# A hybrid retention and attention layer: half of the prompt's gate projections moved from the retention's end into the attention's entry

## The chip, the cores and the metric

The kernel runs on one core of a Trainium2 chip. The metric is the device time of one execution in microseconds (us). TensorE (PE) multiplies matrices, VectorE (DVE), ScalarE (ACT) and GpSimd (POOL) do the elementwise work, and SyncE (SP) issues most of the DMAs. Each engine takes its own instructions strictly in the order in which they were written for it, and stops at the first one whose operands or buffer are not ready.

## The reference, cut to what matters

Two sequences, a sample of 512 tokens and a prompt of 1024, go through the same layer with the same weights:

```python
h = rms_norm(x, norm_g) * (1 + scale) + shift
rq, rk, rv, rg, aq, ak, av, ag = split(h @ w_in)   # 4 x 512, then 512, 128, 128, 512 columns
ret_out = bidirectional_retention(rope(rq), rope(rk), rv)          # 4 heads of 128, chunks of 128
att_out = blocked_gqa(rope(norm(aq)), rope(norm(ak)), av)          # 8 query heads, 2 key heads of 64
mixed = concat([ret_out * silu(rg), att_out * silu(ag)]) @ w_out
y = x + gate * mixed
```

The columns `ag` are the attention's gates. The kernel computes them transposed: a 128-row tile of gate columns by 512 tokens at a time.

## The kernel before, in words

Everything is float32. A product is made of three fast matmuls on operands that are split in a high part and a remainder (`mm3`, lines 148 to 151: high by high, high by low, low by high). A weight is therefore loaded raw by DMA, cast to its high part on ACT (L139), and its remainder is made by a subtract on DVE or POOL (L140). `load_w` does this for 256 columns in four pieces; the tiles stand in a ring of two (`wring`).

`sequence` is called for the sample (nt = 4 query tiles of 128) and then for the prompt (nt = 8). For the prompt it runs through these stages:

1. Four retention heads. Head h's projections are woven with the core of head h-1 (`ret_core`: state sums `pst`, transposes `pk`/`pq`, scores `psc`, outputs `po`, then `pm`, the transposes of the normalised result, once per block of 512 tokens). The last head's core has no following head; it is woven with the attention's gate projections, `gates(rp, "rt1")`. These are 192 matmuls into the banks `pag`, in two weight tiles (`jj`) by two groups of 512 tokens (`g`) by two banks. After each bank comes `silu_gate`: a tanh on ACT (L362) and a combining step on DVE (L363). The results stay in `gs`, and are read in `normalise`.
2. `kvq_units`: keys, values and the first queries (`pkv`, `paq`). Then `ln_tables()` (L305) loads the activation tables that hold both logarithm and exponential, after the last tanh written so far.
3. The entry into the attention: the work of the attention is a list of steps in rounds (half-steps, eight per query tile), and the steps before round `turn` are woven with `q_rest`, which projects the remaining queries (`paq`). When the entry ends, the pools of the weights and of the normalised input are released and the DMAs of the output weights `wo` start into that memory (`read_wo`, at round `turn`).
4. The steady attention, eight query tiles of eight rounds. `st_unit`: scores `pT`, then their exponential `p` on ACT (L925), then row sums on DVE and POOL (L930, L933). `nat_units`: scores `pn` of the tile ahead, whose row maxima DVE takes (L870). `pv_pair`: `po`. After a tile, `normalise`: the logarithm (L962) and the exponential (L963) of the row sums on ACT, the product with the gates on DVE (L968, L969). Then `gate_out` splits the result into `Mh` and `Ml`, and sixteen `out_step`s of three matmuls each (bank `py`) multiply the tile with `wo`. The out-projection of one tile is the filler of PE during the attention of the next.

The order on each engine is the order of the code after weaving; within a round a priority sorts the steps. `weave(units, n, steps, m, lead)` takes one unit and then as many steps as keep the two lists level.

The lines that the change touches are the order of the queries (`qorder`, L338), `gates` (L760 to 777), its call beside the last core (L804), `turn` (L1025), the rounds of `gate_out` and `out_step` (L1054, L1061), and the weave of the entry's second part (L1094).

Of the kernel before, what the change touches and what calls it, by code (L numbers as in the profile page):

```python
# [37 lines left out]
PLEAD = 3  # L38
# [42 lines left out]
def hybrid_layer_kernel(ctx: ExitStack, tc: tile.TileContext, a: dict, y_prompt: bass.AP, y_sample: bass.AP):  # L81
# [23 lines left out]
    def slot(name):  # L105
        return slots.tile([P, 1024], F32, tag="slot", name=name)
# [46 lines left out]
    def load_w(wring, name, segs, wpool=None):  # L153
        w = (wpool or wring).tile([P, KD, 2, 256], F32R, tag="w", name=name)
        for _ in load_w_steps(wring, w, name, segs):
            pass
        return w
# [116 lines left out]
    def iter_steps(fns):  # L274
        for fn in fns:
            fn()
            yield

    def weave(units, n, steps, m, lead=0):
        done = 0  # L280
        for i, _ in enumerate(units):
            while steps is not None and done * (n - lead) < (i + 1 - lead) * m:
                if next(steps, steps) is steps:
                    steps = None
                done += 1
        if steps is not None:
            for _ in steps:
                pass
# [27 lines left out]
    def sequence(r, nt, first):  # L316
        tg = "ps"[r]
        ng = nt // 4
        ntok = nt * P
        x_in, y_out = xs[r], ys[r]  # L320
        with ExitStack() as sctx:
# [13 lines left out]
            order = [2 * tp + i for tp in tps for i in range(2)]  # L335
            kv = {}
            QPRE = hpair if first else 1
            qorder = [(half, tp) for half in range(2) for tp in tps[:QPRE]] + [(half, tp) for tp in tps[QPRE:] for half in range(2)]  # L338

            def open_kv():  # L340
                kvp = sctx.enter_context(pool(f"kv{tg}", bufs=1, reuse_waits="tile"))
# [156 lines left out]
            with ExitStack() as rctx:  # L498
# [258 lines left out]
                        S.mul(mT[:, h, b * 512 : (b + 1) * 512], pm2, gnT[:, h : h + 1])  # L757
                        yield

                def gates(pl, tag):  # L760
                    gs.extend(slot(f"g{tg}{i}") for i in range(2 * ng))
                    for jj in range(2):
                        segs = [(2816 + v * 256 + (2 * jj + i) * DH, DH) for i in range(2) for v in range(2)]
                        w = load_w(wring, f"wg{tg}{jj}", segs)
                        for g in range(ng):
                            for i in range(2):
                                pj = bank(f"pag{tg}{g}{jj}{i}")
                                wc = slice(i * P, (i + 1) * P)
                                c = slice(i * 512, (i + 1) * 512)
                                for k in range(KD):  # L770
                                    mm3(pj, w[:, k, 0, wc], w[:, k, 1, wc], hh[g][:, k, :], hl[g][:, k, :],
                                        k == 0, k == KD - 1)
                                    if k == 3:
                                        yield
                                silu_gate(pl, gs[g * 2 + jj][:, c], pj, [512], f"a{tg}{g}{jj}{i}", tag, 1)
                                yield
# [18 lines left out]
                for h in range(RH + 1):  # L795
                    if h < RH:
                        sls = [slot(f"s{tg}{h}_{i}") for i in range(nt // 2)]
                        units, n = head_units(h, sls), 2 * nt
                    else:
                        wctx.close()  # L800
                        if first:
                            units, n = kvq_units(rctx.enter_context(pool(f"pa{tg}", bufs=2, reuse_waits="tile"))), 2 * nt
                        else:
                            units, n = gates(rp, "rt1"), 8 * ng  # L804
                    extra, m = itertools.islice(gsteps, GSTEPS.get(h, 0)) if first else iter(()), nsteps
                    if first:
                        m += GSTEPS.get(h, 0)
                    weave(units, n, merge(prev, nsteps, extra, m - nsteps), m + ((2, 3)[r] if h == RH else 0))
                    if h == 0:
                        decay_tables()  # L810
                    if first and h < RH:
                        for j in range(sum(WOH[:h]), sum(WOH[: h + 1])):
                            with tc.issue_after(acts["w"].ins):
                                split_wo(wst, j)
                    if h < RH:
                        prev = ret_core(h, sls)
# [162 lines left out]
            def gate_out(t):  # L979
                d = st8[t]  # L980
                if "Mh" not in d:
                    gate_ret(t)
                o, Mh, Ml = d["o"], d["Mh"], d["Ml"]
                split(S.copy, V, Mh[:, 4:8, :], Ml[:, 4:8, :], o.rearrange("p (j q) -> p j q", j=4))
# [37 lines left out]
                        nc.gpsimd.dma_start(y_out[t * P : (t + 1) * P, :], x)  # L1022


            per_ = turn = nt  # L1025
            rounds = {}

            def at_round(rd, prio, fn):
                rounds.setdefault(rd, []).append((prio, fn))

            for n, t in enumerate(order):
                b = n * per_
                hb = b - per_
                prev = st8[order[0]] if n == 1 else {}
                if n:
                    at_round(hb - nt // 2, 8, lambda t=t: prep_split(t))
                    at_round(hb - 1, 6, lambda t=t: prep_T(t))
                if nt == 4:
                    for h in range(QH):
                        at_round(hb + h // 2, 4, lambda t=t, h=h, prev=prev: nat_head(t, h, prev))  # L1040
                else:
                    for k, units, paired in NATS:
                        at_round(hb + k, 4, lambda t=t, z=units, y=paired, prev=prev: nat_units(t, z, y, prev))
                for v in range(2):
                    at_round(b - 2 + v, 7.5, lambda t=t, v=v: fill_q2(t, v))
                    at_round(b - nt // 2 if v == 0 else b - 1, 7, lambda t=t, v=v: mid(t, v))
                    at_round(b - 1 + v, 2.5 if v else 5, lambda t=t, v=v: mid_t(t, v))
                for u in range(nt):
                    at_round(b + u, 1, lambda t=t, u=u: st_unit(t, u))
                    if u % 2:  # L1050
                        at_round(b + 4 * (u // 4 + 1), 3, lambda t=t, u=u: pv_pair(t, u // 2))
                at_round(b + per_, 3.2, lambda t=t: row_sums(t))
                at_round(b + per_, 8.5, lambda t=t: normalise(t))
                at_round(b + per_ + 1, 9, lambda t=t: gate_out(t))  # L1054
                if t == final:
                    at_round(b + per_ - 2, 9, lambda t=t: gate_ret(t))
                    at_round(b + per_ + 1, 10, lambda: final_steps(0))
                    at_round(b + per_ + 2, 10, lambda: final_steps(4))
                    continue
                for u in range(16):  # L1060
                    rd = b + per_ + 3 + u * nt // 16  # L1061
                    at_round(rd if first else min(rd, nt * per_), 0.5 if rd < nt * per_ or first else 4, lambda t=t, u=u: out_step(t, u))
            if first:
                def ahead():
# [10 lines left out]
            with ExitStack() as bctx:  # L1075
                ra = run_rounds_list(rounds, -100, turn)
                if first:
                    pools["at"] = sctx.enter_context(pool(f"at{tg}", bufs=2, reuse_waits="tile"))
                    pb = bctx.enter_context(pool(f"pb{tg}", bufs=2, reuse_waits="tile"))
                    prep_split(order[0])  # L1080
                    prep_T(order[0])
                    weave(itertools.chain(q_rest(pb, tps[hpair], hpair), gates(pb, "tg")), 4 * (nt // 2 - QPRE) + 8 * ng,
                          iter_steps(ra), len(ra), LEAD)
                else:
                    nb = sum(len(rounds[rd]) for rd in rounds if rd < PTURN)
                    with pool(f"pb0{tg}", bufs=2, reuse_waits="tile") as pb:
                        prep_split(order[0])
                        prep_T(order[0])
                        weave(q_rest(pb, tps[QPRE], hpair - QPRE), 4 * (hpair - QPRE), iter_steps(ra[:nb]), nb + 1)
                    hpools.pop().release()  # L1090
                    pools["q2"] = sctx.enter_context(pool(f"q2{tg}", bufs=1, reuse_waits="tile"))
                    pools["at"] = sctx.enter_context(pool(f"at{tg}", bufs=2, reuse_waits="tile"))
                    pb = bctx.enter_context(pool(f"pb{tg}", bufs=2, reuse_waits="tile"))
                    weave(q_rest(pb, tps[hpair], hpair), 4 * hpair, iter_steps(ra[nb:]), len(ra) - nb, PLEAD)  # L1094
                if first:
                    ln_tables()
            for p_ in reversed(hpools):
# [37 lines left out]
```

## Time and profile before

| | |
|---|---|
| time of three runs | 959.77, 952.63, 959.35 us (median 959.35) |
| the profiled execution | 954.35 us, of which the span from first to last instruction is 952.4 |
| busy in the span | PE 912.2 us (96%), DVE 546.5 (57%), POOL 396.1 (42%), ACT 336.7 (35%) |
| TensorE's granted clock | 0.992 of full speed on average |

A row of the timeline gives the start, the duration, the engine, the line, the operation, what it writes and reads, the count, and in brackets how long the engine stood idle before it and what ended that. The instructions of PE overlap; the distance between two starts is what one costs (0.23 us for a 512-column matmul whose own duration reads 0.39). An L number is a line of the kernel before; after the change, lines behind 338 stand one lower on the page, and those behind some 800 two lower.

### The profile page before, as it was taken

To read this page: it belongs to the slowest core of one execution; us is meant where nothing else is said; L and a number is where in the kernel's file an instruction comes from. 1 tells how busy PE (TensorE), PEld (TensorE's weight loads), DVE (VectorE), ACT (ScalarE), POOL (GpSimd) and SP (SyncE) were. 2 spreads that over 40 slices of the span, in tenths; PEclk is the share of its full clock that TensorE was granted. 3 is DMA by queue.
4 is the path that set the end of the run, shared out by engine and by line. 5 is a ranking of instruction groups with operands and counts; after the bars stand their busy time and mean duration, and the time that the engine had idled before them with its cause. 6 is when DMAs were issued, how large, how long until landed. Compare 5 with 4: busy or idle time off the path is not lost. (4 is left out here: it accounts for less than half of the span.)

```text
span 952.4 us, 15494 instructions
## 1 busy us (share of the span) xinstructions
PE 912.2 (96%) x6177; PEld 763.5 (80%) x6177; DVE 546.5 (57%) x972; ACT 336.7 (35%) x582; POOL 396.1 (42%) x346
## 2 busy tenths in 40 slices
PE   4899898999999999999999999999999999999998
PEld 2789798997676799999999998899965656665666
DVE  2475556677753493443525443245887878786833
ACT  3352232343535452232222232233143434343331
POOL 4233354455437673232302211035575546453551
PEclk9999999999999999999999999999999999999999
DMA  9964778214742521111002110110017011101111
GB/s 266 272 202 144 250 214 298 72 46 139 287 159 74 182 85 45 45 45 45 24 22 46 45 45 26 45 51 7 12 45 331 5 41 44 45 23 45 45 45 44
DMA packets 95683, 92.98 MB, mean 98 GB/s; under 512 B 23502, under 2 KB 84858, under 8 KB 92540
## 3 DMA queue, kind: packets, MB, share of 16 engines
q1 hardware_dynamic: 92876, 77.85, 26.8%
q0 software_dynamic: 2736, 14.16, 3.7%
q8 instruction: 48, 0.79, 0.4%
q14 instruction: 23, 0.19, 0.1%
HBM read 77.30 MB, written 14.68 MB: 97 GB/s over the span
## 5 line engine op out<-in xcount | busy, mean ns | idle before, releaser
L925 ACT ACTIVATE pp<-pTp 128x1024 f32<-128x1024 f32 x64 | 65.6, 1026 | 118.8 <-PE pTp L922 100.4
L870 DVE TENSOR_REDUCE nmhp<-pnp 128x2 f32<-128x1024 f32 x64 | 75.5, 1215 | 38.4 <-PE pnp L865 38.4
L933 POOL TENSOR_TENSOR accp<-accp,pp 128x512 f32<-128x512 f32 x48 | 64.9, 1351 | 19.9 <-ACT pp L925 18.3
L149 PE MATMUL pvgp<-wvgp,hhp 128*128 128x256 f32 x224 | 65.0, 290 | 0.0
L149 PE MATMUL pqkp<-wqkp,hhp 128*128 128x256 f32 x224 | 64.6, 288 | 0.0
L150 PE MATMUL pvgp<-wvgp,hhp 128*128 128x256 f32 x224 | 64.3, 287 | 0.0
L151 PE MATMUL pvgp<-wvgp,hlp 128*128 128x256 f32 x224 | 63.9, 285 | 0.0
L151 PE MATMUL pqkp<-wqkp,hlp 128*128 128x256 f32 x224 | 63.6, 284 | 0.0
L150 PE MATMUL pqkp<-wqkp,hhp 128*128 128x256 f32 x224 | 63.3, 283 | 0.0
L942 PE MATMUL pop<-pp,VVp 128*64 128x512 f32 x256 | 58.7, 599 | 0.0
L149 PE MATMUL pyp<-wo,Mhp 128*128 128x512 f32 (+1 forms) x136 | 53.9, 396 | 0.2 <-DVE ygp L1019 0.2
L150 PE MATMUL pyp<-wo,Mhp 128*128 128x512 f32 (+1 forms) x136 | 51.7, 380 | 0.0
L151 PE MATMUL pyp<-wo,Mlp 128*128 128x512 f32 (+1 forms) x136 | 51.6, 379 | 0.0
L933 DVE TENSOR_TENSOR accp<-accp,pp 128x512 f32<-128x512 f32 x48 | 42.7, 890 | 14.5 <-ACT pp L925 14.0
L637 POOL TENSOR_TENSOR sp<-rt1p,rt2p 128x512 f32<-128x512 f32 x16 | 22.9, 1428 | 57.1 <-DVE rt2p L634 57.1
L911 PE MATMUL pTp<-Q1Tp,kkp 128*128 128x512 f32 x128 | 41.4, 404 | 1.6 <-DVE nmhp L870 1.6
L942 PEld LDWEIGHTS pop<-pp,VVp 128*64 128x64 f32 x256 | 16.9, 136 | 32.4 <-issue 29.4
L149 PEld LDWEIGHTS pqkp<-wqkp,hhp 128*128 128x128 f32 x224 | 42.8, 191 | 0.0
L150 PEld LDWEIGHTS pqkp<-wqkp,hhp 128*128 128x128 f32 x224 | 42.8, 191 | 0.0
L149 PEld LDWEIGHTS pvgp<-wvgp,hhp 128*128 128x128 f32 x224 | 42.7, 191 | 0.0
L151 PEld LDWEIGHTS pqkp<-wqkp,hlp 128*128 128x128 f32 x224 | 42.7, 191 | 0.0
L150 PEld LDWEIGHTS pvgp<-wvgp,hhp 128*128 128x128 f32 x224 | 42.7, 191 | 0.0
(456 smaller groups left out, 2857.3 us busy)
## 6 DMA issues: line engine op xcount, KB each, us to landing
wo<-wod SPq DMA_DIRECT2D x16, 1024.0 KB, 14.7
wa<-in_w_ada_dram SPq DMA_DIRECT2D x16, 512.0 KB, 6.6
wod<-woz POOLq DMA_DIRECT2D x8, 1024.0 KB, 6.4
gr<-in_w_ada_dram SPq DMA_DIRECT2D x16, 256.0 KB, 5.0
xn<-in_x_prompt_dram SPq DMA_DIRECT2D x8, 512.0 KB, 7.6
xrp<-in_x_prompt_dram SPq DMA_DIRECT2D x8, 512.0 KB, 3.8
out_dram<-xrp POOLq DMA_DIRECT2D x7, 512.0 KB, 3.0
xs<-in_x_sample_dram SPq DMA_DIRECT2D x4, 512.0 KB, 6.6
```

What stands on the lines that cost most here:

```text
L149: T.matmul(out, lh, rh, start=first, stop=False)
L150: T.matmul(out, lh, rl, start=False, stop=False)
L151: T.matmul(out, ll, rh, start=False, stop=last)
L637: G.tensor_tensor(qk, t1, t2, op=ALU.add)
L870: V.tensor_reduce(d["nmh"][:, n, 2 * pr : 2 * pr + 2], pn.rearrange("p (i k) -> p i k", i=2), AX.X, ALU.max, negate=True)
L911: T.matmul(pT[:, i * 512 : (i + 1) * 512], kk[v][:, kb], st8[t]["Q1T"][:, hs, :].rearrange("p h q -> p (h q)"), start=True, stop=False)
L925: d["exp", u] = S.activation(p, pT, AF.Exp)
L933: d["sum", v] = E.tensor_tensor(acc, acc, p[:, i * 512 : (i + 1) * 512], op=ALU.add)
L942: m = T.matmul(d["po"][v * DH : (v + 1) * DH, :], VV[:, 2 * kp + i, v, :], ps[v][:, i * 512 : (i + 1) * 512], start=(kp + i == 0), stop=(2 ...
```

## The change

The gate projections of the prompt's first 512 tokens (group 0) leave the retention's end: `gates` takes a list of groups, the call beside the last core keeps group 1, and a second call for group 0 follows `q_rest` in the entry's weave. Since the weight tiles in the ring have been overwritten by then, the second call loads them again. The entry runs to round 11 instead of 8, with the start of `wo`, the first `gate_out` and all `out_step`s of the prompt three rounds later. The order of the second half's queries changes so that one weight tile is done with before the other, which frees its place in the ring.

```diff
+            qorder = [(half, tp) for half in range(2) for tp in tps[:QPRE]] + [(half, tp) for tp in tps[QPRE:hpair] for half in range(2)]
+            qorder += [(half, tp) for half in range(2) for tp in tps[hpair:]] if not first else [(half, tp) for tp in tps[hpair:] for half in range(2)]
...
-                def gates(pl, tag):
-                    gs.extend(slot(f"g{tg}{i}") for i in range(2 * ng))
+                def gates(pl, tag, groups=range(ng)):
+                    if not gs:
+                        gs.extend(slot(f"g{tg}{i}") for i in range(2 * ng))
...
-                        w = load_w(wring, f"wg{tg}{jj}", segs)
-                        for g in range(ng):
+                        w = load_w(wring, f"wg{tg}{jj}{groups[0]}", segs)
+                        for g in groups:
...
-                            units, n = gates(rp, "rt1"), 8 * ng
+                            units, n = gates(rp, "rt1", range(1, ng)), 8 * (ng - 1)
...
-            per_ = turn = nt
+            per_ = nt
+            turn = nt if first else nt + 3
...
-                at_round(b + per_ + 1, 9, lambda t=t: gate_out(t))
+                at_round(max(b + per_ + 1, turn), 9, lambda t=t: gate_out(t))
...
-                    rd = b + per_ + 3 + u * nt // 16
+                    rd = b + per_ + (3 if first else 6) + u * nt // 16
...
-                    weave(q_rest(pb, tps[hpair], hpair), 4 * hpair, iter_steps(ra[nb:]), len(ra) - nb, PLEAD)
+                    weave(itertools.chain(q_rest(pb, tps[hpair], hpair), gates(pb, "tg", range(1))), 4 * hpair + 8, iter_steps(ra[nb:]), len(ra) - nb, PLEAD)
```

Three places show how the instructions move. The first is PE at the retention's end, block 0 of the last head. Before, between the last output product `pop_0` and the first transpose `pmp_0` of the normalised block stand 25 gate matmuls:

```order
L739 MATMUL pop_0_6385<-R1p_6231,qd1p_0_6348 128x128
L739 MATMUL pop_0_6385<-sp_1_5537,sTp_0_6370 128x128
L151 MATMUL pagp_6372<-hhp_3527,wgp_6188 128x512
L149 MATMUL pagp_6454<-hhp_3526,wgp_6425 128x512
...
L151 MATMUL pagp_6454<-hhp_3526,wgp_6425 128x512
L501 MATMUL pmp_0_6467<-identr,mxp_0_6405 128x128
L501 MATMUL pkp_1_6488<-identr,sp_2_5538 128x128 x2
```

After the change they follow each other directly:

```order
L740 MATMUL pop_0_6344<-R1p_6231,qd1p_0_6320 128x128
L740 MATMUL pop_0_6344<-sp_1_5537,sTp_0_6327 128x128
L502 MATMUL pmp_0_6411<-identr,mxp_0_6364 128x128
L502 MATMUL pkp_1_6417<-identr,sp_2_5538 128x128 x2
L502 MATMUL pkp_1_6417<-identr,sp_3_5539 128x128 x2
```

For block 1, four gate matmuls stand between `pop_1` and `pmp_1` where there were ten.

The second place is ACT in a steady tile, around the logarithm and the exponential of the row sums. Before:

```order
L948 COPY op_8737<-pop_8610 128x512
L962 ACTIVATE pLp_8739<-pLp_8739 128x512
L963 ACTIVATE pLp_8739<-pLp_8739 128x512
L925 ACTIVATE pp_8766<-pTp_8761 128x1024
L139 CAST Mhp_8994<-mTp 128x512
```

After the change, each of the two has a table load ahead of it:

```order
L950 COPY op_9207<-pop_9093 128x512
L964 ACT_TABLE_LOAD
L964 ACTIVATE pLp_9209<-pLp_9209 128x512
L965 ACT_TABLE_LOAD
L965 ACTIVATE pLp_9209<-pLp_9209 128x512
L927 ACTIVATE pp_9231<-pTp_9226 128x1024
```

This is so in all eight tiles of the prompt, and one more load stands ahead of the first tanh in the entry: 17 loads that the program did not have.

The third place is PE behind the last gate matmul in the entry (`pag`, line 149 to 151). After the change 23 rows of the attention alone stand between it and the first out-projection `pyp`; these are the first six and the last three:

```order
L151 MATMUL pagp_7861<-hhp_3526,wgp_7765 128x512
L913 MATMUL pTp_7905<-Q1Tp_7480,kkp_6522 128x512 x2
L924 MATMUL pTp_7905<-Q2Tp_7821,k2p_6524 128x512 x2
L913 MATMUL pTp_7913<-Q1Tp_7480,kkp_6521 128x512 x2
L924 MATMUL pTp_7913<-Q2Tp_7750,k2p_6523 128x512 x2
L867 MATMUL pnp_7922<-kkp_6521,Q1Tp_7816 128x512 x2
...
L913 MATMUL pTp_7999<-Q1Tp_7480,kkp_6522 128x512 x2
L924 MATMUL pTp_7999<-Q2Tp_7821,k2p_6524 128x512 x2
L149 MATMUL pyp_8012<-wo_7938,Mhp_7957 128x512
```

Before, the stretch of the attention without filler lies between the last query projection `paq` and the first `pyp`; the transposes `pnm` and `pq1` of the first two tiles lie in it:

```order
L151 MATMUL paqp_7668<-wqp_6969,hlp_3528 128x256
L865 MATMUL pnp_7731<-kkp_6634,Q1Tp_7551 128x512 x2
L911 MATMUL pTp_7779<-Q1Tp_7180,kkp_6634 128x512 x2
L922 MATMUL pTp_7779<-Q2Tp_7556,k2p_6636 128x512 x2
L887 MATMUL pnmp_7788<-identr,nmp_7553 4x128
L844 MATMUL pq1p_7791<-identr,Q1p_7710 128x128 x8
```

What moved: 96 rows of `pag` stand in the entry behind `paq`, and those transposes lie among them. Without filler stand the second half of the first tile's scores and the `pn` of the next, three rounds later than before.

## Rows read from the trace of the kernel before

**Rows 1.** The page, part 1: busy time of each engine, its share of the span.

```profile
PE 912.2 (96%) x6177; PEld 763.5 (80%) x6177; DVE 546.5 (57%) x972; ACT 336.7 (35%) x582; POOL 396.1 (42%) x346
```

**Rows 2.** Busy time by stage: retention's end, entry, steady attention; clock, DMA share, GB/s last.

```profile
559.30:616.80 57.50, 56.65 (x306) 48.14 (x305) 22.08 (x42) 15.76 (x30) 8.36 (x8) 1.00 0.16 48
655.00:711.00 56.00, 55.60 (x387) 46.54 (x386) 44.47 (x77) 14.31 (x20) 30.72 (x28) 1.00 0.03 8
731.00:933.00 202.00, 199.17 (x903) 125.57 (x902) 144.59 (x165) 80.19 (x100) 102.04 (x79) 1.00 0.11 38
```

**Rows 3.** Timeline of PE, block 1 at the retention's end.

```profile
607.22 0.39 PE L739 MATMUL pop<-sp,sTp 128*128 128x128 f32 x2
607.37 0.48 PE L151 MATMUL pagp<-hhp,wgp 128*128 128x512 f32 x1
...
609.30 0.40 PE L150 MATMUL pagp<-hlp,wgp 128*128 128x512 f32 x1
609.53 0.40 PE L151 MATMUL pagp<-hhp,wgp 128*128 128x512 f32 x1
610.78 0.33 PE L501 MATMUL pmp<-identr,mxp 128*128 128x128 f32 x1 [0.85 <-DVE mxp L748]
```

**Rows 4.** Timeline of ACT, DVE and POOL there: the chain from `pop` to `mxp`.

```profile
607.65 0.60 ACT L741 ACTIVATE sqp<-pop 128x512 f32<-128x512 f32 x1 [5.08 <-PE pop L739]
...
609.33 1.01 POOL L127 TENSOR_TENSOR r_retp<-m_retp,mhalf 128x4 f32<-128x4 f32 x1
...
610.38 1.13 DVE L748 SCALAR_TENSOR_TENSOR mxp<-pop,r_retp,sp 128x128 f32<-128x128 f32 x4 [1.42 <-POOL r_retp L127]
```

**Rows 5.** PE at the sample's retention end, and the busy times just behind.

```profile
159.17 0.49 PE L739 MATMUL pos<-R1s,qd1s 128*128 128x128 f32 x2 [3.02 <-DVE qd1s L716]
...
159.60:163.00 3.40, 3.40 (x18) 3.40 (x17) 2.18 (x4) 0.00 (x0) 0.59 (x1) 0.50 0.78 246
```

**Rows 6.** Timeline of PE in the entry and behind it: rows with idle before them; one stretch.

```profile
691.44 0.50 PE L865 MATMUL pnp<-kkp,Q1Tp 64*128 64x512 f32 x2 [0.35 <-DVE Q2Tp L888]
...
712.02 0.85 PE L844 MATMUL pq1p<-identr,Q1p 128*128 128x128 f32 x8 [0.43 <-DVE nmhp L870]
...
714.73 0.22 PE L887 MATMUL pnmp<-identr,nmp 128*4 128x128 f32 x1 [0.74 <-DVE nmp L882]
...
721.14 0.73 PE L911 MATMUL pTp<-Q1Tp,kkp 128*128 128x512 f32 x2 [1.09 <-DVE nmhp L870]
...
722.88 1.22 PE L911 MATMUL pTp<-Q1Tp,kkp 128*128 128x512 f32 x2 [0.52 <-DVE nmhp L870]
...
722.80:726.20 3.40, 3.32 (x8) 2.68 (x9) 3.37 (x6) 1.64 (x2) 1.44 (x2) 0.50 1.01 424
```

**Rows 7.** Groups by line between 559 and 711 us: the gate matmuls and one weight's preparation.

```profile
L149 PE MATMUL pagp<-hhp,wgp 128*128 128x512 f32 x64 | 26.0, 406 | 0.0
...
L140 DVE TENSOR_TENSOR wgp<-wgp1r,wgp 128x512 fp32r<-128x512 f32 x2 | 3.1, 1570 | 0.6 <-ACT wgp L139 0.6
...
L139 ACT CAST wgp<-wgp1r 128x512 fp32r<-128x512 f32 x4 | 2.2, 628 | 0.0
```

**Rows 8.** The page, parts 5 and 6: the row maxima; the output weights' issues, time to landing.

```profile
L870 DVE TENSOR_REDUCE nmhp<-pnp 128x2 f32<-128x1024 f32 x64 | 75.5, 1215 | 38.4 <-PE pnp L865 38.4
...
wo<-wod SPq DMA_DIRECT2D x16, 1024.0 KB, 14.7
```

**Rows 9.** Timeline of ACT around the prompt's one table load for the tanh.

```profile
360.71 1.28 ACT L362 ACT_TABLE_LOAD   x1
362.01 0.39 ACT L362 ACTIVATE tg_p<-p0p 128x256 f32<-128x256 f32 x1
```

**Rows 10.** Timeline of ACT and PE in one steady tile.

```profile
783.63 0.58 ACT L963 ACTIVATE pLp<-pLp 128x512 f32<-128x512 f32 x1
786.13 1.03 ACT L925 ACTIVATE pp<-pTp 128x1024 f32<-128x1024 f32 x1 [1.92 <-PE pTp L922]
...
806.48 0.85 PE L844 MATMUL pq1p<-identr,Q1p 128*128 128x128 f32 x8 [0.37 <-POOL accp L933]
```

More of the change, by code (lines that the diff above doesn't have):

```diff
@@ L337, in sequence @@
             QPRE = hpair if first else 1
-            qorder = [(half, tp) for half in range(2) for tp in tps[:QPRE]] + [(half, tp) for tp in tps[QPRE:] for half in range(2)]
+            qorder = [(half, tp) for half in range(2) for tp in tps[:QPRE]] + [(half, tp) for tp in tps[QPRE:hpair] for half in range(2)]
+            qorder += [(half, tp) for half in range(2) for tp in tps[hpair:]] if not first else [(half, tp) for tp in tps[hpair:] for half in range(2)]
             def open_kv():
```

## The prediction

> **What bounds the kernel now.** First the busy times: PE works 912.2 of 952.4 us, no other engine more than 57% [rows 1]. So a change that leaves PE's own work as it is can only win or lose PE's idle time and clock. Second the busy times by stage. In the 57.5 us of the retention's end PE is busy 56.65, in the 56 us of the entry 55.60, in the 202 us of steady attention 199.17 [rows 2]. Third the rows of PE with idle time before them, for what ended it: one wait of 0.85 us at the retention's end [rows 3], five waits of 0.35 to 1.09 us in the entry and behind it [rows 6], some 0.4 us per steady tile [rows 10]. The other engines matter through the chains that end these waits.
>
> The profiled execution took 954.35 us, 1.95 more than its span, and lies 5.0 below the median 959.35. The three timed runs scatter from 952.63 to 959.77; the mean over the four executions is 956.5. I make the sum as a difference and set it on that mean. A difference within 1% (9.5 us) can't be told from no change.
>
> **The change, part by part.**
>
> *Work.* PE has the same matmuls as before; 96 of the 192 gate matmuls, 0.23 us from start to start (609.30 to 609.53, [rows 3]), move: 22 us leave one place and enter another. That alone is zero. The second load of two weight tiles adds 2 MB of DMA in 32 issues on SP; in the entry the DMA share is 0.03 [rows 2], SP has the rope tables before and between them, and `wo` comes only after, so I cost it at nothing. It adds eight casts on ACT (2.2 us per four), four subtracts on DVE and four on POOL (3.1 us per two on DVE) [rows 7]. ACT is busy 14.3 of the entry's 56 us and takes that. DVE is busy 44.5 of the 56 [rows 2]: it is the engine that can't hide 6.2 us at will.
>
> *Retention's end: +6.8.* Between the last `pop` and the first `pmp` lies a chain over three engines: square on ACT at 607.65, then a sum on DVE, root on POOL at 609.33, product on DVE at 610.38 [rows 4], and `pmp` at 610.78. From 607.37, where PE is free behind `pop`, that is 3.4 us. Ten gate matmuls cover 2.5 of it, and 0.85 shows [rows 3]. In block 0 of before 25 gate matmuls (5.7 us) cover all. The change takes all 25 from block 0: 3.3 us bare. In block 1 it leaves four (0.9 us): 2.5 bare, up to 3.4 if DVE is late, since a subtract of the next weight now stands ahead of its product. The state sums and scores of the two blocks lose their filler as well and wait on ACT's copies, each at most an ACT operation of 0.6 us as in [rows 4] and its handover: I estimate 1.1 us for both. Together 3.3 + 3.4 + 1.1 = 7.8, less the 1.0 that was there, is 6.8. The range is 3 (chains partly overlap) to 9. The trace has the same place without filler: the sample's retention end, where PE waits 3.02 us for one such chain [rows 5].
>
> *Clock: +2.* Behind that wait of 3.02 us the granted clock is 0.50 for the stretch from 159.6 to 163.0 [rows 5], 1.2 in place of 2.4 GHz. Behind the waits of 1.09 and 0.52 us at 721 it is 0.50 for 3.4 us as well [rows 6]. PE loses half of such a stretch, 1.7 us, where it has work. Two bare waits of 3.3 us can bring two such stretches; a wait that falls into the second costs nothing twice. I take +2, from 0 to 3.4.
>
> *Entry: -2.7.* The five waits there sum to 0.35 + 0.43 + 0.74 + 1.09 + 0.52 = 3.1 us, and the half clock behind them costs 1.6 [rows 6]: 4.7 to be won, if gate matmuls stand beside the maxima and the transposes. Against this stand 23 rows without filler behind the last gate matmul, some 10 us in which each scores unit waits for an exponential, and DVE makes the maxima (1.2 us each, [rows 8]) behind three subtracts; I estimate 2.0 us of new waits, about half of one subtract (1.57 us, [rows 7]) and one maximum. `wo` is asked for at the end of the gates; a piece lands 14.7 us after issue in the median [rows 8], where all eight share the queues, the first of them earlier; the first `py` needs the first piece alone, about 10 us on, and I cost it at nothing. The range goes from -4.7 to +3, if the two subtracts push DVE's queue for the queries (load 44.5 of 56, plus 3) into PE's path.
>
> *Steady tiles: +1.4.* In before each tile has a wait of about 0.4 us ahead of `pq1` [rows 10]; the later out-projection puts a combine and a subtract ahead of the row sums on DVE, +0.27 for five of them. The new table loads come on top: two per tile, 1.28 us each by the only one on view [rows 9], 16 in all, 20.5 us of ACT. ACT idles 1.92 us between the exponential of the row sums and the next `p` [rows 10], so of 2.57 us some 0.65 are left, and PE stands one or two units behind ACT, with margins of 0.25 to 0.4 us in the consumers `pn` and `pT`, and out-projection as filler. I take the loads at zero, since the row nearest to the case shows ACT free there; the bound on the other side is 16 x 1.28 = 20.5.
>
> After the load at 360.71 the tanh starts at 362.01, 1.30 us later [rows 9]: nothing beyond the load itself. The Trainium skill (ScalarE: Activation LUTs, What ACT_TABLE_LOAD costs) agrees on 1283 ns, but adds a drain of about 1380 ns, 2.66 us for every switch. By it two switches would take 5.3 us, 2.8 more per tile than in my sum, some 20 us over the tiles; the row speaks against the drain here. The same page's next section, on table sets as the batching unit, says that logarithm and exponential share one set and that calls should be batched by set; the change breaks this, since the tanh now comes behind the common set's load.
>
> *Tail: 0.* Twelve out-steps instead of six stand behind the last tile's scores; they were to be done anyway, and cover the last chain with its two loads better than six did.
>
> **Sum:** 6.8 + 2.0 - 2.7 + 1.4 = +7.5 us. On the profiled execution that is 961.9, on the mean of the four 964.0, on the median 966.9. I predict 964.
>
> **The rivals.**
>
> *A. The table loads reach PE* (0.22). ACT works in order: exponentials of `pT`, which free PE's score banks, stand behind the loads. If the 0.65 us left per tile grow, because `Mh` and two `p` follow at once, one load per tile becomes bare: 8 x 1.28 = 10.3 more, +17.8, 974. All bare would be 984. It decides from the point where ACT's lag exceeds the 0.4 us of the consumers. Against it: ACT is busy 80 of 202 us [rows 2], and DVE's and PE's orders there leave time. By the drain that the Trainium skill states (ScalarE: Activation LUTs, What ACT_TABLE_LOAD costs) it would be likelier; the rows show none.
>
> *B. The entry wins all, the retention loses little* (0.25). The end of the retention: the core's steps may meet their operands later anyway, +3, and no half clock behind it; the entry gives its 4.7. Sum -1.7, or 955: faster than before, though not measurably. For it: the entry's waits are real and in the trace. Against: the order leaves no row between `pop_0` and `pmp_0`. It decides at a retention loss below 4.7. A gain of over 1% would need 9.5 us of idle time, and the stages that the change touches hold 1 + 4.7 + 2.8 in all, so that I give it little.
>
> *C. No net effect of the tables, but the entry becomes DVE's* (inside the forecast's range): +3 instead of -2.7, 970.
>
> **Chances and range.** The forecast with C has 0.53, A 0.22, B 0.25. Of the forecast, from +2 to +13, some 0.35 lies above 9.5; of A nearly all; of B none, and of B and the scatter of the runs some 0.08 below -9.5. So faster 0.08, same 0.52, slower 0.40. The range goes from B on the lowest run (952.6 - 1.7 = 951) to one bare load per tile on the highest (959.8 + 17.8 = 977.6): 951 to 977.
>
> **What would show it.** In the profile after: PE waits of about 3 us on `mxp` twice between 585 and 615, with a clock of 0.50 behind them; no waits over 0.5 us on `nmh` and `nm` among the gate matmuls of the entry, and some behind them; 17 more table loads on ACT, and in each steady tile no other new wait of PE, with the 0.4 us ahead of `pq1` grown to 0.7. I am wrong if a wait of PE on `pp` or `pL` stands in every steady tile (A), if the retention's end grows by less than 3 us (B), or if PE waits on `wgp` or `Q1` in the entry.

## The result: 1% slower, with a wait of 1.2 us per steady tile at a place that the prediction did not look at

| | before | after |
|---|---|---|
| median of 11 runs | 953.54 us | 964.74 us |
| lowest to highest | 950.56 to 959.77 | 962.15 to 967.69 |
| ratio, 95% interval | | 1.0102 [1.0082, 1.0121] |
| span of the profiled execution | 952.4 us | 963.4 us |

The prediction said 964.0 us (951 to 977), a difference of +7.5. Measured are 964.7 and, by the ratio, +9.7. That the two times lie so close is luck: the sum was set on 956.5 us, 3.0 above the median of before's eleven runs, and its difference was 2.2 too small. At 1.0102 the result lies on the edge between no change and slower by over 1%.

The two profiles can't be subtracted as they stand. The first gate matmul of the prompt starts at 559.26 us before and at 561.84 after, and up to there the program is the same. In the eleven kernels profiled here it starts between 556.75 and 563.60. So all sums below count from that start. Each stage begins with a row of PE: the first gate matmul, the first key projection `pkv` (616.81 before, 603.50 after), the first query projection `paq` (640.94, 629.58), the row sums `pL` of the second tile (750.51, 753.54) and of the seventh (907.08, 914.34), the end of the span. The moved matmuls are added or taken off at 0.2275 us each (about the distance between two of their starts): 96 gate matmuls, and the 18 of the out-projection that stand ahead of the second tile's row sums before and behind them after.

| stage | measured | predicted |
|---|---|---|
| retention's end | +6.0 | +6.8 |
| half clock behind it, to the first `paq` | +1.9 | +2.0 |
| entry, to the second tile's row sums | -3.4 | -2.7 |
| five steady tiles, 156.57 to 160.80 us | +4.2 | +1.4 |
| tail | -0.3 | 0 |
| sum | +8.5 | +7.5 |

The sum is that of one execution of each kernel; +9.7 comes from all timed runs. Two of the rows hold something else beside what they are named for. Of the +1.9 behind the retention's end, 0.4 is no clock: of the four transposes `pm` of block 1, three stood ahead of the first `pkv` before and stand behind it after. So the retention's end itself is +6.4, and the half clock 1.5. And of the entry's -3.4, some 1.6 is the half clock behind two of the waits of before [rows 6], which this execution of after did not have.

This is what PE waited for from 561 us on in the kernel after; the columns are engine and line, what it waited for, us in total, times, longest:

```profile
PE pyp L149 <- DVE ygp L1021: 6.0, 5, 1.2
PE pmp L502 <- DVE mxp L749: 5.9, 2, 3.2
PE pTp L913 <- DVE nmhp L872: 0.9, 1, 0.9
PE pstp L694 <- ACT vdp L678: 0.4, 1, 0.4
PE pscp L724 <- ACT qTp L713: 0.4, 1, 0.4
PE pnp L867 <- DVE nmhp L872: 0.4, 1, 0.4
PE pTp L913 <- ACT pp L927: 0.3, 1, 0.3
```

Rows two, four and five are the retention's end, as the sum had them. The wait ahead of `pq1` [rows 10] is gone from the list. In its place the first row is the largest of all, and the prediction had none there: five times 1.2 us, the out-projection `pyp` waiting for `ygp`, the combine that empties its bank. These 6.0 us, less the five waits of 0.4 that went, are 4.0 of the +4.2 of the five steady tiles. The rows of PE's timeline in which these waits show:

```profile
586.10 0.39 PE L740 MATMUL pop<-sp,sTp 128*128 128x128 f32 x2
589.65 0.33 PE L502 MATMUL pmp<-identr,mxp 128*128 128x128 f32 x1 [3.16 <-DVE mxp L749]
...
603.42 0.33 PE L502 MATMUL pmp<-identr,mxp 128*128 128x128 f32 x1 [2.70 <-DVE mxp L749]
...
733.98 0.73 PE L913 MATMUL pTp<-Q1Tp,kkp 128*128 128x512 f32 x2 [0.26 <-ACT pp L927]
...
740.52 0.73 PE L913 MATMUL pTp<-Q1Tp,kkp 128*128 128x512 f32 x2 [0.86 <-DVE nmhp L872]
...
773.76 0.50 PE L149 MATMUL pyp<-wo,Mhp 128*128 128x512 f32 x1 [1.20 <-DVE ygp L1021]
```

The first two answer to [rows 3]: 0.85 us there, 3.16 and 2.70 here. The next two stand in the unfilled stretch behind the last gate; with the 0.37 of the one `pn` they sum to 1.5 us, and replace the five waits of [rows 6]. The half clock shows in the busy times just behind the second long wait (last four columns: POOL's busy time, granted clock, DMA share, GB/s); it begins at 604.82, so that the mean of the stretch is 0.62:

```profile
604.00:607.40 3.40, 3.40 (x21) 3.40 (x21) 1.97 (x3) 0.72 (x1) 1.93 (x2) 0.62 0.74 219
```

DVE's timeline ahead of the wait at 773.76 says why the bank came late:

```profile
769.62 3.49 DVE L872 TENSOR_REDUCE nmhp<-pnp 128x2 f32<-128x1024 f32 x3 [3.19 <-PE pnp L867]
773.02 0.68 DVE L1021 TENSOR_TENSOR ygp<-pyp,gmod 128x512 f32<-128x512 f32 x1
```

The three row maxima of the next tile (3.5 us) stand ahead of the combine. The pool that holds `po` and `py` has two banks (`8 - 2 * nwide`, wide ones being three), given out in turn. After the change the order is `po`, `py` first half, `py` second half, `po`, so the first half of the next tile gets the very bank that the second half has just filled, and PE can't start it before DVE has emptied it. The order alone doesn't make the wait: by the rounds in the code it is the same at 5 and 7 in place of 6, and neither has this wait (e5 and e4 below). What the rows show of 6 alone is that the combine stands behind the maxima while PE has only one unit of scores (`pT`, 1.1 us) between the two halves.

The table loads are where the prediction had them. ACT's timeline in the same tile:

```profile
786.89 1.28 ACT L964 ACT_TABLE_LOAD   x1 [0.31 <-PE pLp L956]
788.19 0.58 ACT L964 ACTIVATE pLp<-pLp 128x512 f32<-128x512 f32 x1
788.79 1.28 ACT L965 ACT_TABLE_LOAD   x1
790.08 0.58 ACT L965 ACTIVATE pLp<-pLp 128x512 f32<-128x512 f32 x1
790.57 1.02 ACT L927 ACTIVATE pp<-pTp 128x1024 f32<-128x1024 f32 x1
```

Each load takes 1.28 us, and the next function starts within 20 ns of its end, as in [rows 9]. The only waits on ACT's exponentials in the list above are 0.3 us once, in the entry.

### The profile page after: what moved, and what is told of

Same layout as the page of the kernel before. It is cut to its first block, busy times and chain, and to the rows that moved or that the text cites. A ratio compares the mean times of both kernels' runs of the same rounds, so it can differ in the third digit from the quotient of the medians.

```text
span 963.4 us, 15592 instructions
## 1 busy us (share of the span) xinstructions
PE 913.4 (95%) x6177; PEld 762.9 (79%) x6177; DVE 551.1 (57%) x976; ACT 360.9 (37%) x607; POOL 399.9 (42%) x350
## 4 chain that ended last, share of the span: by engine, by line
PE 85%; DMA 4%; DVE 4%; ACT 2%; issue 2%; SPq 2%; POOL 1%; ACTq 0%; POOLq 0%; DVEq 0%
PE pop L944 6%; PE pyp L149 3%; PE pTp L913 3%; PE pqkp L151 3%; PE pvgp L150 3%; PE pqkp L149 3%; PE pTp L924 3%; PE pvgp L151 3%; PE pvgp L149 3%; PE pqkp L150 3%; PE pyp L150 3%; PE pyp L151 3%; PE pnp L867 2%; PE pop L740 2%; PE paqp L149 2%
## 5 line engine op out<-in xcount | busy, mean ns | idle before, releaser
L1022 POOL TENSOR_TENSOR xrp<-ygp,xrp 128x512 f32<-128x512 f32 x14 | 20.3, 1453 | 76.0 <-DVE ygp L1021 76.0
L935 DVE TENSOR_TENSOR accp<-accp,pp 128x512 f32<-128x512 f32 x48 | 47.3, 985 | 7.2 <-ACT pp L927 6.4
L151 PEld LDWEIGHTS pvgp<-wvgp,hlp 128*128 128x128 f32 x224 | 42.7, 191 | 0.0
```

Of the source, the lines that this page charges most:

```text
L151: T.matmul(out, ll, rh, start=False, stop=last)
L935: d["sum", v] = E.tensor_tensor(acc, acc, p[:, i * 512 : (i + 1) * 512], op=ALU.add)
L1022: G.tensor_tensor(x[:, c], yg, x[:, c], op=ALU.add)
```

## The experiments

The table gives the ratio to the kernel before and, by the marks above, each stage's difference from before in us. "Tile" is the mean of five steady tiles.

| kernel | ratio, 95% interval | retention's end and clock | entry | five tiles | tail | tile |
|---|---|---|---|---|---|---|
| before | 1 | 0 | 0 | 0 | 0 | 31.31 |
| after | 1.0102 [1.0082, 1.0121] | +7.9 | -3.4 | +4.2 | -0.3 | 32.16 |
| e1 tables late | 1.0108 [1.0070, 1.0147] | +10.2 | -2.4 | +4.4 | -0.3 | 32.19 |
| e2 shift alone | 1.0037 [1.0012, 1.0061] | 0.0 | -1.5 | +4.3 | -0.3 | 32.17 |
| e3 gates alone | 1.0050 [1.0026, 1.0075] | +7.5 | -1.7 | 0.0 | 0.0 | 31.32 |
| e4 shift 7 | 1.0171 [1.0131, 1.0211] | +6.4 | -2.8 | +10.1 | +0.6 | 33.33 |
| e5 shift 5 | 1.0006 [0.9984, 1.0029] | +6.4 | -4.3 | -2.7 | -0.5 | 30.78 |
| e8 shift 5, gates as before | 0.9943 [0.9922, 0.9964] | 0.0 | -1.2 | -2.6 | -0.5 | 30.79 |
| e9 shift 5, half the gates | 1.0037 [1.0017, 1.0057] | +4.6 | -0.3 | -2.6 | -0.5 | 30.79 |
| e11 shift 4, gates as before | 0.9953 [0.9934, 0.9972] | 0.0 | -1.4 | -2.6 | 0.0 | 30.79 |
| e12 shift 5, one step later | 0.9949 [0.9930, 0.9968] | +3.4 | -4.3 | -2.6 | -0.5 | 30.79 |

"Shift" is the number in the round of `out_step`: 3 before, 6 after. Each stage is read from one execution. The profiles of before, e8, e9 and e11 have a half clock in the entry, some 1.6 us; the others have none there, and look that much better in this column. In e1 the lines behind 829 have the numbers of before, in e12 those behind the retention stand nine lower than in after.

**e1, the tables loaded behind the last gate.**

```diff
-            if not first:
-                ln_tables()
...
-                if first:
-                    ln_tables()
+                ln_tables()
```

> The changed kernel with the load of the common logarithm and exponential tables moved behind the entry's last gate, so that the tables are loaded 3 more times than in the kernel before, not 17. Theory (the loads lie in ACT's idle time, no PE wait of the changed kernel's steady tiles names ACT): steady tile stays at 32.24 us, time as the changed kernel's, ratio 1.008 to 1.012. Rival A (late exponentials delay DVE and through it the out-projection's bank): the tile falls back towards 31.4 us, about 4 to 5 us less, ratio 1.005.

The loads at the logarithm and the exponential fall from 16 to 2. The tile stays at 32.19 us and the list of waits keeps its first rows:

```profile
PE pyp L149 <- DVE ygp L1019: 6.0, 5, 1.2
PE pmp L502 <- DVE mxp L749: 5.9, 2, 3.2
```

The ratio is the changed kernel's, within the intervals. For the steady tiles rival A of the prediction falls: two loads of 1.28 us per tile on ACT cost PE nothing measurable. e5 and e8 below say the same, with the loads and without them (30.78 and 30.79 us). In the entry the load that e1 moved isn't free. The trace has six loads in all, two more than before, and the last one stands behind the last gate, where PE has no filler:

```profile
727.23 1.28 ACT L307 ACT_TABLE_LOAD   x1
...
PE pTp L911 <- ACT pp L925: 1.6, 2, 0.9
```

PE waits 1.6 us there for the exponentials, where the kernel after has 0.3, and the entry is 1.0 us longer. The 2.4 us by which the retention's end is longer here come from the clock, told below.

**e2 and e3, the two halves of the change.** e2 undoes the gates' move and keeps the shift; e3 undoes the shift.

```diff
# e2, against after
-                            units, n = gates(rp, "rt1", range(1, ng)), 8 * (ng - 1)
+                            units, n = gates(rp, "rt1"), 8 * ng
...
-                    weave(itertools.chain(q_rest(pb, tps[hpair], hpair), gates(pb, "tg", range(1))), 4 * hpair + 8, iter_steps(ra[nb:]), len(ra) - nb, PLEAD)
+                    weave(q_rest(pb, tps[hpair], hpair), 4 * hpair, iter_steps(ra[nb:]), len(ra) - nb, PLEAD)
# e3, against after
-            turn = nt if first else nt + 3
+            turn = nt
...
-                    rd = b + per_ + (3 if first else 6) + u * nt // 16
+                    rd = b + per_ + 3 + u * nt // 16
```

> Gates all beside the last retention core as before; only the entry's end and the out-projection three rounds later. Theory (the steady tile's new wait of 1.2 us is the out-projection's bank, given back only behind three row maxima on DVE, and comes from the shift alone): steady tile 32.2 us, +4.2 over five tiles, no cost at the retention's end, entry's unfilled stretch not better than before, 0 to +3: +4 to +7, ratio 1.004 to 1.008. Rival (the gates in the entry or the table loads make the steady wait): steady tile 31.4, ratio 1.000 to 1.003.

> Gates of the first 512 tokens in the entry as in the changed kernel; the entry's end and the out-projection where they were before. Theory: retention's end and half clock +7.9 as in the changed kernel, steady tile 31.4 us with the 0.4 us wait ahead of the transposed queries, entry between 0 and -3.4: +4.5 to +8, ratio 1.005 to 1.008, although 17 table loads are there. Rival A (loads reach PE): steady tile above 32 and ratio above 1.010.

e2's ratio lies just under the range given for the theory, since its entry gained 1.5 us where 0 to +3 was expected; e3's lies at the lower end of its own. PE's waits in e2, its first row, then two of e3's:

```profile
PE pyp L149 <- DVE ygp L1021: 6.0, 5, 1.2
```

```profile
PE pmp L502 <- DVE mxp L749: 5.9, 2, 3.2
PE pq1p L846 <- POOL accp L935: 1.8, 5, 0.4
```

The steady tile's wait of 1.2 us belongs to the shift alone (e2 has no gates in the entry and no added table load), the 5.9 us at the retention's end to the gates alone. e3 has all 17 loads and the tile of before, 31.32 us. The entry's gain needs both. By the marks it is -1.5 in e2, -1.7 in e3 and -3.4 with both, but none of the three has the half clock of before. Counted by PE's waits alone, 3.1 us before, the entry has 2.8 in e2, 2.6 in e3 and 1.5 in after.

**e4, the out-projection one round later still.**

```diff
-                    rd = b + per_ + (3 if first else 6) + u * nt // 16
+                    rd = b + per_ + (3 if first else 7) + u * nt // 16
```

> The changed kernel with the out-projection one round later still (7 in place of 6), so that the tile's second half again takes the bank that the first half gave back at the phase in which it did before. Theory (bank handed over behind three row maxima): the 1.2 us wait goes, steady tile 31.4 to 31.7, 3 to 4.5 us less than the changed kernel, ratio 1.005 to 1.007. Rival (DVE has no room for any shifted order, or the table loads): steady tile 32.2 or more, ratio 1.010.

The expected gain didn't come: the rival came true, and worse. The wait for the bank did go (0.2 us once), but a larger one took its place ahead of `pq1`, in four tiles 8.3 us. A tile's row of PE, then DVE's order in it:

```profile
773.35 0.85 PE L846 MATMUL pq1p<-identr,Q1p 128*128 128x128 f32 x8 [2.05 <-DVE nmhp L872]
```

```profile
763.17 3.48 DVE L872 TENSOR_REDUCE nmhp<-pnp 128x2 f32<-128x1024 f32 x3 [3.23 <-PE pnp L867]
767.20 0.69 DVE L935 TENSOR_TENSOR accp<-accp,pp 128x512 f32<-128x512 f32 x1 [0.54 <-ACT pp L927]
767.81 0.68 DVE L1021 TENSOR_TENSOR ygp<-pyp,gmod 128x512 f32<-128x512 f32 x1
768.41 0.68 DVE L140 TENSOR_TENSOR Mlp<-mTp,Mhp 128x512 fp32r<-128x512 f32 x1
769.01 1.78 DVE L935 TENSOR_TENSOR accp<-accp,pp 128x512 f32<-128x512 f32 x1
770.72 1.35 DVE L878 CAST Q2Tp<-Q1Tp 64x256 fp32r<-64x256 f32 x1
772.00 1.21 DVE L872 TENSOR_REDUCE nmhp<-pnp 128x2 f32<-128x1024 f32 x1
```

From the three maxima to the fourth DVE has 10 us without a gap of more than 0.54, and `pq1` needs the wide bank that the fourth empties. Combine and subtract stand inside. So one theory is offered for before, after and e4: this stretch of DVE is the tight one, and it costs what is put into it. Before, one combine stood in it, at 0.4 us per tile. The trace of before names a step of POOL for that wait [rows 10], but the fourth maximum ends 0.14 us ahead of the `pq1` at 806.48, as it does in e4 (773.21 to 773.35):

```profile
802.62 0.68 DVE L1019 TENSOR_TENSOR ygp<-pyp,gmod 128x512 f32<-128x512 f32 x1
...
805.13 1.21 DVE L870 TENSOR_REDUCE nmhp<-pnp 128x2 f32<-128x1024 f32 x1
```

Not all of e4's +10.1 is DVE's: two of the four waits have a half clock behind them, at 806.07 and 874.34, and these two tiles are 1.3 and 1.6 us longer than the other two, which take 33.0 us. One of the two stretches:

```profile
806.07:809.48 3.41, 3.15 (x13) 2.79 (x14) 3.31 (x6) 1.01 (x1) 2.43 (x3) 0.50 0.60 171
```

**e5, one round earlier than the change.**

```diff
-                    rd = b + per_ + (3 if first else 6) + u * nt // 16
+                    rd = b + per_ + (3 if first else 5) + u * nt // 16
```

> The changed kernel with the out-projection one round earlier (5 in place of 6; the entry still ends three rounds later). The second half of a tile's out-projection then ends ahead of the three row maxima, and its bank is given back before DVE takes them. Theory: the 1.2 us wait of the changed kernel goes, and DVE's stretch up to the transposed queries is one combine shorter than before, so the 0.4 us wait goes too: steady tile 31.0 us (32.24 in the changed kernel, 31.39 before), some 6 us less than the changed kernel, ratio 1.002 to 1.004. Rival (DVE's total, not the order, sets the tile; the wait reappears ahead of the transposed queries as it did one round later): 31.4 to 33 us, ratio 1.006 to 1.015.

The combine and the subtract now stand ahead of the three maxima, in time that DVE had free (its idle before them falls from 3.19 to 1.53 us):

```profile
760.82 0.68 DVE L1021 TENSOR_TENSOR ygp<-pyp,gmod 128x512 f32<-128x512 f32 x1
761.42 0.68 DVE L140 TENSOR_TENSOR Mlp<-mTp,Mhp 128x512 fp32r<-128x512 f32 x1
762.02 1.76 DVE L935 TENSOR_TENSOR accp<-accp,pp 128x512 f32<-128x512 f32 x1
765.32 3.48 DVE L872 TENSOR_REDUCE nmhp<-pnp 128x2 f32<-128x1024 f32 x3 [1.53 <-PE pnp L867]
```

Both waits are gone, and the tile takes 30.78 us, below the 31.0 expected (the expectations' 32.24 and 31.39 are means of four tiles). The ratio, 1.0006, lies below the 1.002 to 1.004 expected. PE now has the 16 `po` matmuls (761.19 to 764.84) between the two halves of the out-projection, time for the combine at 760.82. One digit takes the change from 1.0102 to 1.0006.

**e8 and e11, the shift without the gates.** e8 is e2 with 5 in place of 6. e11 is e2 with 4, and `turn` at nt + 2.

> All gates beside the last retention core as before, the entry's end three rounds later, the out-projection two rounds later (5). Theory: nothing lost at the retention's end, entry about 1.5 us better as in the kernel with the shift alone, steady tile 31.0 us, -2: together -3.5 us, ratio 0.995 to 0.998, faster than both kernels. Rival (the gain of the entry needs the gates there; steady tile no better than before): ratio 0.999 to 1.003.

> All gates beside the last retention core as before, the entry's end two rounds later, the out-projection one round later (4). Theory (it is the place of combine and subtract in DVE's order that makes the wait): they stand within DVE's stretch up to the transposed queries, so the wait there is between the 0.4 us of before and the 2.1 us of the kernel with the out-projection four rounds later: steady tile 31.4 to 32.5, ratio 0.999 to 1.007. Rival (later is better in itself, as the entry's end moves): ratio 0.996 to 0.998, like the kernel with 5.

e8 is faster than both kernels: 0.9943, a little better than the 0.995 to 0.998 expected. In e11 the rival's number came true: the tile is e8's, and the ratio lies below both ranges. Its reason, that later is better in itself, doesn't hold, since 6 and 7 are worse. The stretch theory isn't contradicted, but the combine's place was expected wrongly: in e11's profile it comes behind the fourth maximum (772.61, the maximum at 771.22), outside the stretch. DVE's order in the built program would have shown that beforehand. This reading was made after the run, and no further run tries it.

**e9 and e12, the retention's end.** e9 leaves half of the moved matmuls (those of the second weight tile) in the entry. e12 keeps all of them there and moves one step of the last core: block 0's transposes of `mx` come behind the transposes `pk` and `pq` of block 1.

```diff
# e9, against e5: the call beside the retention leaves out one of four (group, weight tile) pairs, the entry computes it
-                            units, n = gates(rp, "rt1", range(1, ng)), 8 * (ng - 1)
+                            units, n = gates(rp, "rt1", late=((0, 1),)), 8 * ng - 4
...
-                    weave(itertools.chain(q_rest(pb, tps[hpair], hpair), gates(pb, "tg", range(1))), 4 * hpair + 8, iter_steps(ra[nb:]), len(ra) - nb, PLEAD)
+                    weave(itertools.chain(q_rest(pb, tps[hpair], hpair), gates(pb, "tg", range(1), (1,))), 4 * hpair + 4, iter_steps(ra[nb:]), len(ra) - nb, PLEAD)
# e12, against e5, in ret_core
+                        if held:
+                            held.pop()()
                         kT = rp.tile([P, 512], F32, tag="rkT", name=f"kT{nm}")
...
+                        def transposed(b=b, nm=nm, mx=mx):
+                            pm2 = bank(f"pm{nm}")
+                            for i in range(4):
+                                tr(pm2[:, i * P : (i + 1) * P], mx[:, i * P : (i + 1) * P])
+                            S.mul(mT[:, h, b * 512 : (b + 1) * 512], pm2, gnT[:, h : h + 1])
...
+                        if not first and h == RH - 1 and b == 0:
+                            held.append(transposed)
+                        else:
+                            transposed()
```

> As the kernel with the out-projection two rounds later, but only half of the moved gate matmuls (48) in the entry, the other 48 back beside the retention. Theory (what counts at the retention's end is the number of rows between the last output product and the first transpose, 3 in block 0 and 5 in block 1 here, not the amount of work): waits of about 2.6 and 2.3 us on the normalised block, retention's end and clock +5 to +7, ratio 1.001 to 1.004. Rival (the cost goes with the work moved): half of 7.9, +4, ratio 0.998 to 1.000.

> The kernel with the out-projection two rounds later (5) and all 96 moved gate matmuls in the entry, with one step of the last retention core later: the transposes of block 0's normalised result come behind those of block 1's queries and keys. With it 8 gate matmuls stand between the last output product and the first such transpose in block 0 (none before the edit) and 6 in block 1 (4). Nothing else changes. Theory (the wait is the chain's 3.4 us less the rows that stand in it, 0.23 us each): 3.2 - 1.8 = 1.4 us in block 0 and 2.7 - 0.5 = 2.2 in block 1, together 3.6 in place of 5.9, ratio 0.996 to 0.999 (1.0006 without the edit). Rival (PE lacks work at the retention's end altogether, so the wait comes back at another place of it): the stretch from the first gate matmul to the first query projection is as long as without the edit, ratio 1.000 to 1.002.

In e9 the two waits are 2.70 and 2.00 us (2.6 and 2.3 expected): half the work moved costs 80% of the 5.9 us. The stage came to +4.6, less than the theory's 5 to 7, since no half clock followed here. The rival's 4 was half of 7.9 with clock; half of the 6.4 without clock (e5) is 3.2. The entry of e9 gains only 0.3 us. It has one new wait of PE, and the chain behind it runs through the two table loads of the first tile's normalisation:

```profile
722.22 1.28 ACT L964 ACT_TABLE_LOAD   x1
723.51 0.58 ACT L964 ACTIVATE pLp<-pLp 128x512 f32<-128x512 f32 x1
724.11 1.28 ACT L965 ACT_TABLE_LOAD   x1
725.41 0.58 ACT L965 ACTIVATE pLp<-pLp 128x512 f32<-128x512 f32 x1
...
726.95 0.69 DVE L971 TENSOR_TENSOR op<-op,pLp 128x512 f32<-128x512 f32 x1
...
727.79 0.70 PE L913 MATMUL pTp<-Q1Tp,kkp 128*128 128x512 f32 x2 [2.46 <-DVE op L971]
```

By the trace `pT` waits for the step at L971, the last to read the bank of the row sums. The wait, 2.46 us, is about as long as the two loads (2.57), and a half clock follows it at 728.73. So the entry has about what it had before: 2.7 us of waits against 3.1, and a half clock in both. In e5, with 48 more gate matmuls as filler there, the same step waits for nothing. So here the loads do seem to reach PE, once; that is read from the trace, and no run of this kernel with its loads elsewhere shows it.

In e12 the waits, and both places in the timeline:

```profile
589.56 0.33 PE L502 MATMUL pmp<-identr,mxp 128*128 128x128 f32 x1 [1.67 <-DVE mxp L752]
...
600.91 0.33 PE L502 MATMUL pmp<-identr,mxp 128*128 128x128 f32 x1 [1.78 <-DVE mxp L752]
```

3.4 us in place of 5.9 (3.6 expected), with the same work in the same stage, which is 3.0 us shorter. The ratio falls from 1.0006 to 0.9949, just below the range expected; that is more than 3.0 us, but within the two intervals. So 3.0 of the 6.4 us were lost for want of rows between `pop` and `pmp`, and not for want of work. The waits fall with the rows in them: in block 0 from 3.16 us without a row to 2.70 with three and 1.67 with eight, in block 1 from 2.70 with four to 2.00 with five, 1.78 with six and the 0.85 of before with ten. Even so the move of the gates brings nothing: e12 has them in the entry, e8 has not, and the two come to -4.0 and -4.4 us by the marks (0.9949 and 0.9943).

## Why the prediction held, and where it didn't

**Retention's end, +6.8: right, 0.4 too much.** It measured +6.4, with the 0.4 that fell behind the mark. Block 0 waited 3.16 us (3.3 forecast), block 1 2.70 (2.5 to 3.4, of which the sum took 3.4), the two ACT copies 0.4 each (1.1 for both). e2, e8 and e11, which have no gates moved, show 0.0 at this place; e12 moves the wait with the rows in it. This is shown.

**Clock, +2: it came to 1.5, and that is chance.** In the kernel after only the second long wait has a half clock behind it. In e1's profile, whose program is the same there, the first has one too. The stretch behind the first wait in after, and in e1:

```profile
590.00:594.00 4.00, 3.60 (x27) 3.15 (x26) 2.28 (x5) 1.66 (x3) 0.00 (x0) 1.00 0.00 0
```

```profile
586.00:590.00 4.00, 3.96 (x18) 3.56 (x17) 1.72 (x3) 1.82 (x3) 0.00 (x0) 0.50 0.00 0
```

The granted clock is 1.00 in the one and 0.50 in the other, behind the same wait of 3.16 us. That is the 2.4 us between the two retention stages. Five profiles have the same order of PE at this place, and what they have there above the 6.4 is half clock: 1.5 us in after, 3.9 in e1, 1.1 in e3, none in e4 and e5. The forecast's 0 to 3.4 covers all but e1.

**Entry, -2.7: right, -3.4.** The five waits of before went, 3.1 us, and the half clock behind them, 1.6; the new waits behind the last gate are 1.5 us where 2.0 was forecast, and no wait on `wo` appeared. The 1.6 is chance in part: the waits of 0.98 us at the same place in e8 and e2 have a half clock behind the one (720.30) and none behind the other.

**Steady tiles, +1.4: the step that failed.** It put the later combine and subtract at +0.27 us for five tiles ahead of `pq1` [rows 10], and took the table loads at zero. No row gives the 0.27; the prediction states it without working. The loads are zero in the steady tiles (e1, e3, e5 against e8). But the wait at `pq1` vanished, and 1.20 us stood at `pyp`: the step asked what the combine delays behind it in DVE's queue, and not who waits for the combine itself, which gives back a bank that PE wants at once. It measured +4.2, three times the term. e2 shows that the shift alone makes it, e5 that one round less takes it away. The wait that the step had in mind came one round later, in e4: 2.05 us ahead of `pq1`, not 0.7.

**Rivals.** A (the loads reach PE) is refuted for the steady tiles by e1; e9's entry shows a place where the loads seem to reach PE. By the Trainium skill (ScalarE: Activation LUTs, What ACT_TABLE_LOAD costs) each switch would add a drain of about 1380 ns; the rows above show the next function 10 to 20 ns behind the load's end, and it is so in all 16 of these loads. B (the retention loses little) was wrong for this order; e12 shows an order in which it loses 3.4 instead of 6.4. Its sum of -1.7 also leaves out the +1.4 of the steady tiles. C did not occur: the entry gained.

What stays open: no run tries the loads in e9's entry, and none sets the combine alone to another place in DVE's order, which would try the stretch theory directly. A kernel with e12's order, half of the gates and the shift of 5 was not run.

## What to carry to other kernels

Work taken from beside a chain costs by the rows that stood inside its waits, not by its amount: count them in the order of the built program, and try to move one of the chain's own steps (e12: 2.4 us of 5.9). When a periodic consumer is shifted, write down the order in which the buffers of its pool are given out, what the waiting engine has to do in between, and where the release falls in the queue of the engine that empties the buffer: a shift of 5, 6 or 7 rounds made a tile of 30.8, 32.2 or 33.0 us here (without half clock). A profile pair is compared from the first row that differs, since the common part before it scattered by 7 us; and a stage's difference is split into waits and clock, since the clock behind the same wait differs from one execution to the next.

## What the runs showed of the hardware that was not expected

The same wait of PE, 3.16 us, was followed by the full clock in one execution and by half of it in another (the windows above), and a wait of 0.98 us at one place likewise (e8 and e2). So a term for the clock is a range even where the wait is certain. And VectorE's add of 128x512 takes 0.69 us at 767.20 and 1.78 us at 769.01 in the same tile of e4; what shares its time was not isolated.
